# A convolution that stores the first image of its first pair in two halves

## The chip, the cores and the metric

The kernel runs on one core of one Trainium2 chip. The metric is the device time of one execution, in microseconds (us), less being better. A profiled execution is shown by its span (from the first to the last instruction that the profiler records) and its own device time, which is a little longer than the span.

## What is computed

A 3x3 convolution with a border of zeros: 16 images of 64 channels and 64 x 64 pixels in float32, 128 output channels.

```
x_pad = np.pad(x, ((0, 0), (0, 0), (1, 1), (1, 1)))
output[b, co] += weight[co, ci, kh, kw] * x_pad[b, ci, kh:kh+h, kw:kw+w]     # for all b, co, ci, kh, kw
```

The input is 16 MB, the output 32 MB.

## The kernel before

The images go through in eight **pairs** (`NP`, loop in line 128). A pair fills the 128 partitions: image 0 of the pair has its 64 channels on partitions 0 to 63, image 1 on 64 to 127. Each pair has four **blocks** (line 138) of 8 row pairs, that is, 16 output rows. The row direction uses a short (Winograd) form: the sum of two neighbouring input rows, made beforehand into `ss`, goes through the middle weights once and serves an even and an odd output row. A block therefore has three groups of matmuls in float16 on TensorE (line 168): U from `ss`, A and Bt from the rows themselves in `xs`. ScalarE copies U out of PSUM into `ut` (line 182); VectorE adds A and U into the even output rows (line 190), then Bt and U into the odd ones (line 193), for image 0 first and image 1 second. The result lies in `ot`, one float32 tile of 2 MB for each image.

**Loads.** SyncE issues the weights and the first three pairs as raw float32 (x0, x1, x2; lines 41 to 47, 2 MB each) before anything else. ScalarE and GpSimd cast them to float16 (line 98): x1 during pair 0, x2 piece by piece during pair 1. GpSimd issues the loads of pairs 3 to 7 itself (`load`, line 58), cast on the way from 2 MB of float32 to 1 MB of float16: pairs 3 and 4 early (line 108), pairs 5 to 7 after its sums for pair 2 (line 134). It also makes the sums for each next pair (line 131).

**Stores.** `cuts_of[p]` (line 120) says for each pair, and for each of its two images, after which block which rows are stored: `whole` means all 64 rows after block 3, `halves` means rows 0 to 31 after block 1 and rows 32 to 63 after block 3. Before the change all pairs use `whole` but the last, which uses `halves` for both images. Image 0 is stored by SyncE straight away (line 195). Image 1's store is put on a list, `held`, and issued by ScalarE after its copies of a later block (line 185).

**Queues.** SyncE's transfers (weights, x0 to x2, stores of image 0) share DMA queue 1, in order of issue; ScalarE's stores go through queue 10; GpSimd's casting loads through queue 0. All run on the same 16 DMA engines. On each engine's instruction stream a store waits for the addition that finishes its rows, and the instructions behind it wait with it. SyncE has nothing behind its loads but the stores.

**Buffers.** `opool` has seven 2 MB buffers, which the raw tiles x0 to x2 and the output tiles take in turn. Eight semaphores serve SyncE's and ScalarE's transfers in turn.

Of the kernel before, what the change touches and what calls it, by code (L numbers as in the profile page):

```python
# [13 lines left out]
def kernel(  # L14
# [10 lines left out]
    NP = B // 2  # L25
# [91 lines left out]

    whole = {3: (0, 64)}
    halves = {1: (0, 32), 3: (32, 64)}
    cuts_of = [(whole, whole)] * (NP - 1) + [(halves, halves)]  # L120

    def store(eng, p, b2, ot, lo, hi):
        return eng.dma_start(
# [106 lines left out]
```

## Time and profile before

| | |
|---|---|
| median of 3 runs | 126.69 us (126.62 to 126.82) |
| the profiled execution's own time | 126.58 us |
| its span | 124.8 us |
| TensorE busy | 107.9 us (86% of the span) |
| VectorE busy | 84.6 us (68%) |
| ScalarE busy | 46.5 us (37%) |
| GpSimd busy | 37.5 us (30%) |
| HBM read and written | 17.07 MB and 33.55 MB |
| stores of 2 MB, from issue to landing | median 18.4 us (SyncE), 19.9 us (ScalarE) |
| stores of 1 MB, from issue to landing | median 10.6 us (SyncE), 11.0 us (ScalarE) |

How to read the profile: PE is TensorE, DVE VectorE, ACT ScalarE, POOL GpSimd, SP SyncE; "L193" is line 193 of the kernel. `out<-in` names the tile written and the tile read. "DMA" rows give the busy share of the 16 DMA engines in tenths and the GB/s that landed; a casting load lands half the bytes that it reads. The chain of waits follows the work that ended last back to the start, the timeline lists instructions in order of time (equal ones merged), and the table of stretches gives, for each stretch of time, the busy time and number of instructions of each engine, TensorE's granted clock, the DMA engines' share and the GB/s.

### The profile page before, as it was taken

Reading aid. Unit: us, or ns where it says so; the run is one execution under the profiler, and the core shown is the slowest. Engines: PE = TensorE matmul, PEld = TensorE weight load, DVE = VectorE, ACT = ScalarE, POOL = GpSimd, SP = SyncE. Lnnn points to the kernel's source line nnn. Section 1 sums busy time; section 2 is a strip of 40 time slices with the busy share of each in tenths; the row PEclk is TensorE's granted clock in tenths of the full one; section 3 lists DMA queues with packets and bytes.
Section 4 is the critical chain, followed back from the end, with each engine's and each line's share of the span. In section 5 each row is a group of like instructions: output and inputs, shape, how many; then the busy total and the mean of one; then the engine's idle time right before and its main releaser. Section 6 shows DMA issues by size and latency. Waiting matters only on the chain.

```text
span 124.8 us, 2423 instructions
## 1 busy us (share of the span) xinstructions
PE 107.9 (86%) x984; PEld 49.8 (40%) x984; DVE 84.6 (68%) x135; ACT 46.5 (37%) x78; POOL 37.5 (30%) x28
## 2 busy tenths in 40 slices
PE   0599999999999999999999999999999999990000
PEld 0444444444444444444444444444444444440000
DVE  1019977878877887877777778777877787774000
ACT  4118549966663332433333333333333333330000
POOL 2219780799990006600093002900000000000000
PEclk9999999999999999999999999999999999999555
DMA  4999999999999999999999999999999999999991
GB/s 113 406 425 446 441 315 257 213 155 410 352 352 349 349 378 357 352 344 347 386 339 362 344 357 431 425 436 436 415 425 431 431 425 436 425 415 417 423 407 63
DMA packets 3898, 45.52 MB, mean 365 GB/s; under 512 B 432, under 2 KB 432, under 8 KB 560
## 3 DMA queue, kind: packets, MB, share of 16 engines
q1 hardware_dynamic: 1872, 23.36, 44.7%
q10 hardware_dynamic: 1296, 16.78, 31.7%
q0 software_dynamic: 720, 5.24, 20.8%
q8 instruction: 7, 0.11, 0.3%
q14 instruction: 3, 0.02, 0.0%
HBM read 17.07 MB, written 33.55 MB: 406 GB/s over the span
## 4 chain that ended last, share of the span: by engine, by line
PE 86%; DMA 2%; DVE 1%; issue 1%; POOL 1%; DVEq 0%
PE acc L168 81%; PE warm L91 3%; DMA w_raw<-in_weight_dram 2%; PE wp L85 1%; DVE ot L190 1%; POOL w L52 1%; DVEq L225 0%; DVE ot L193 0%; DVEq L190 0%
## 5 line engine op out<-in xcount | busy, mean ns | idle before, releaser
L168 PE MATMUL acc<-xs,Wt 64*128 64x504 f16 (+3 forms) x768 | 87.0, 373 | 0.0
L168 PEld LDWEIGHTS <-Wt 64*128 64x128 f16 x960 | 46.8, 94 | 56.2 <-issue 0.8
L182 ACT COPY ut<-acc 128x512 f32<-128x512 f32 x64 | 34.4, 589 | 57.1 <-issue 39.3
L190 DVE TENSOR_TENSOR ot<-acc,ut 128x512 f32<-128x512 f32 x64 | 41.2, 685 | 20.9 <-PE acc L168 18.6
L193 DVE TENSOR_TENSOR ot<-acc,ut 128x512 f32<-128x512 f32 x64 | 41.1, 683 | 0.0
L67 POOL TENSOR_TENSOR ss<-xs 128x1024 f16<-128x1024 f16 x10 | 21.0, 2127 | 31.5 <-DMA xs<-in_x_dram 31.2
L168 PE MATMUL acc<-ss,Wt 64*128 64x504 f16 (+1 forms) x192 | 26.0, 377 | 0.0
L98 ACT CAST xs<-x 128x1024 f16<-128x1024 f32 (+1 forms) x10 | 10.5, 1069 | 3.0 <-DMA x<-in_x_dram 3.0
L67 POOL TENSOR_TENSOR ss<-x 128x1024 f16<-128x1024 f32 x4 | 9.4, 2361 | 5.0 <-DMA x<-in_x_dram 5.0
L67 DVE TENSOR_TENSOR ss<-x 128x512 f16<-128x512 f32 x4 | 3.3, 868 | 7.5 <-DMA x<-in_x_dram 7.5
L85 PE MATMUL wp<-ident,w 128*64 128x128 f16 x18 | 1.3, 328 | 4.6 <-POOL w L52 4.6
L98 POOL CAST xs<-x 128x1024 f16<-128x1024 f32 (+1 forms) x2 | 3.0, 1518 | 4.2 <-DMA x<-in_x_dram 4.2
L91 PE MATMUL warm<-blank 128*128 128x400 f32 x6 | 4.1, 854 | 0.0
L85 PEld LDWEIGHTS <-w 128*64 128x64 f16 x18 | 1.1, 209 | 4.6 <-POOL w L52 4.6
L58 POOL DMA_DIRECT2D xs<-in_x_dram x5 | 2.9, 578 | 0.0
L91 PEld LDWEIGHTS warm<-blank 128*128 128x128 f32 x6 | 1.8, 328 | 1.4 <-issue 1.3
L92 ACT CAST Wt<-wp 128x384 f16<-128x384 f32 x1 | 0.5, 479 | 3.3 <-PE wp L85 3.3
L92 ACT ACT_TABLE_LOAD x1 | 1.3, 1283 | 0.7 <-PEq L214 0.7
L52 POOL CAST w<-w_raw 128x576 f16<-128x576 f32 x1 | 0.7, 662 | 2.6 <-DMA w_raw<-in_weight_dram 2.6
L88 DVE MEMSET blank<- 128x400 f32 x1 | 0.4, 392 | 0.9 <-PEq L214 0.9
L103 ACT CAST Wt<-wp 128x384 f16<-128x384 f32 x1 | 0.5, 478 | 0.5 <-DVE Wt L95 0.5
L94 DVE TENSOR_TENSOR Wt<-wp,Wt 128x384 f16<-128x384 f32 x1 | 0.6, 550 | 0.0
(8 smaller groups left out, 1.9 us busy)
## 6 DMA issues: line engine op xcount, KB each, us to landing
out_dram<-ot SPq DMA_DIRECT2D x7, 2048.0 KB, 18.4
out_dram<-ot ACTq DMA_DIRECT2D x7, 2048.0 KB, 19.9
x<-in_x_dram SPq DMA_DIRECT2D x3, 2048.0 KB, 12.0
xs<-in_x_dram POOLq DMA_DIRECT2D x5, 1024.0 KB, 20.4
out_dram<-ot SPq DMA_DIRECT2D x2, 1024.0 KB, 10.6
out_dram<-ot ACTq DMA_DIRECT2D x2, 1024.0 KB, 11.0
w_raw<-in_weight_dram SPq DMA_DIRECT2D x1, 288.0 KB, 3.1
```

The costliest lines, as they stand in the source:

```text
L52: keep(nc.gpsimd.tensor_copy(w16, w_raw))
L58: keep(nc.gpsimd.dma_start(xs[p], x_rows[128 * p : 128 * p + 128, :, :]))
L67: eng.tensor_add(ss[p][:, lo : lo + n, :], v[:, lo : lo + n, 0, :], v[:, lo : lo + n, 1, :])
L85: nc.tensor.matmul(wp[q : q + 64, k * CO : k * CO + CO], w16[:, t::9], ident)
L91: nc.tensor.matmul(warm[:, 0:400], blank[:, 0:128], blank)
L92: keep(nc.scalar.copy(wrow(G1), wps[1]))
L94: keep(nc.vector.tensor_sub(wrow(G21), wps[2], wrow(G1)))
L98: keep(copy(xs[p][:, lo:hi, :], src[:, lo:hi, :]))
L168: nc.tensor.matmul(tiles[b2][:, lo - j0 : hi - j0, c_lo:c_hi], Wt[p0 : p0 + 64, wi, kw, :], rhs, start=i == 0, stop=i == n - 1,)
L182: keep(nc.scalar.copy(ut, U[b2]))
L190: nc.vector.tensor_add(ots[b2][:, j0 : j0 + RB, 0, :], A[b2], us[b2])
L193: nc.vector.tensor_add(ots[b2][:, j0 : j0 + RB, 1, :], Bt[b2], us[b2])
```

## The change

```
     whole = {3: (0, 64)}
     halves = {1: (0, 32), 3: (32, 64)}
-    cuts_of = [(whole, whole)] * (NP - 1) + [(halves, halves)]
+    cuts_of = [(halves, whole)] + [(whole, whole)] * (NP - 2) + [(halves, halves)]
```

For pair 0, image 0, line 195 now issues two stores from SyncE: rows 0 to 31 after block 1 and rows 32 to 63 after block 3, 1 MB each, in place of one store of 2 MB after block 3. Image 1 of pair 0 and all other pairs are stored as before.

## The prediction

> **What bounds the kernel now.** The chain of waits comes first, because it names what ended last among the engines. Its last pieces:
>
> ```profile
> 9.94 101.39 PE acc L168 x948
> ...
> 113.27 0.60 DVE ot L193
> ```
>
> Columns: start, length, what. TensorE works without a hole from 9.94 to 112 us, and VectorE ends at 113.27 + 0.60 = 113.9 us. But the span is 124.8 us: for 10.9 us no engine works. The page's 40 slices say what does:
>
> ```profile
> DVE  1019977878877887877777778777877787774000
> ...
> DMA  4999999999999999999999999999999999999991
> GB/s 113 406 425 446 441 315 257 213 155 410 352 352 349 349 378 357 352 344 347 386 339 362 344 357 431 425 436 436 415 425 431 431 425 436 425 415 417 423 407 63
> ```
>
> The DMA engines are busy from the second slice to the last but one, through the four slices (of 3.1 us) in which VectorE is idle. Is that full speed? Section 3 of the page gives the bytes:
>
> ```profile
> q0 software_dynamic: 720, 5.24, 20.8%
> ...
> HBM read 17.07 MB, written 33.55 MB: 406 GB/s over the span
> ```
>
> The five casting loads (line 58, queue 0) read 10.49 MB and land 5.24 MB, and the GB/s row counts what lands. So where queue 0 runs alone, 215 GB/s stands for 430 read. The stretches of the trace (DMA share and GB/s are the last two columns; PE busy and count come first):
>
> ```profile
> 22.00:25.00 3.00, 3.00 (x34) 1.38 (x32) 2.40 (x5) 2.80 (x5) 2.40 (x2) 1.00 1.05 218
> 25.00:28.00 3.00, 3.00 (x30) 1.36 (x28) 2.34 (x4) 1.85 (x4) 3.00 (x3) 1.00 1.01 153
> 28.00:30.00 2.00, 2.00 (x22) 0.92 (x20) 1.94 (x4) 0.77 (x2) 2.00 (x3) 1.00 1.04 393
> 114.00:120.00 6.00, 0.00 (x0) 0.00 (x0) 0.00 (x0) 0.00 (x0) 0.00 (x0) 0.61 1.02 431
> ```
>
> At 22 to 25 us, 218 landed is 436 read: full. In the end stretch only stores move, at 431: full. 17.07 + 33.55 = 50.62 MB at 431 GB/s is 117.4 us. So **the bytes bound the kernel**, and the remaining 7.4 us of the span are the start, the ragged end (410, 295 and 123 GB/s in the microseconds 120 to 123) and one hole: 25 to 28 us, where 153 GB/s land although the DMA share is 1.01. Its price: (218 - 153) x 3 us = 0.195 MB landed, 0.39 MB read, over 0.431 = **0.9 us**.
>
> What is that hole? Not lack of work: between 27.5 and 28.5 us the trace has 18 more packets of queue 0, and that queue's share stays at 99.3% in 25 to 28 us, with 54 packets where 22 to 25 us had 96. The packets take longer. What is new is the first store:
>
> ```profile
> 23.66 13.15 SPq L123 DMA_DIRECT2D out_dram<-ot  x2
> ```
>
> ```profile
> q0 software_dynamic: 54, 0.44, 99.3%
> q1 hardware_dynamic: 1, 0.02, 1.3%
> ```
>
> The first row (SyncE's issues; two merged, the first at 23.66 us) starts the first 2 MB store; the others (queues in 25 to 28 us: packets, MB, share) show that 4 us later it has written one packet. All packets slow down about 2 us after the first store's issue and recover as its packets appear. ScalarE's first store, issued at 26.86 us, brings no second hole: 28 to 30 us lands 393, with loads among it. I read the hole as the price of the first store into otherwise pure load traffic, paid once.
>
> **The change, part by part.** It removes one 2 MB store (issue 23.66 us) and adds two of 1 MB. No other instruction moves: the order on PE, DVE, ACT and POOL is the same; SyncE has one store more, and the waits that guard reused DMA semaphores shift by one place.
>
> *Issue.* The first half needs the last addition into rows 0 to 31 of image 0, in block 1. VectorE's two additions of line 193 there start at 16.48 us and take 1.29 us; the first, image 0's, ends near 17.1. The store now follows its addition (22.95 + half of 1.28 = 23.6) by under 0.1 us, so the first half issues at about **17.2 us, 6.5 us earlier**; the second stays at 23.66. One more issue costs SyncE 0.33 us, which waits up to 21.1 us between stores: nothing. The shifted semaphores cost nothing either: one is taken again after eight transfers, at the shortest from 75.5 to 113.9 us, and a store lands 25.5 us after its issue at the latest. Behind the waiting first half on SyncE stand only the other stores, all due later. The next one due is the second half, 6.5 us later.
>
> *Queue.* All loads of line 47 and before are already issued, so the first half stands behind the rest of image pair x2 on queue 1. x2 lands at 22.5 us (GpSimd's sums of it start at 22.60 after 4.23 us of waiting), so the half writes from about 21 us on, beside queue 0. In 16 to 19 us queues 0 and 1 moved 42 and 38 packets: they take turns. The half is 128 rows of 8 KB, 8 packets for each of 16 engines; one turn of both is 0.31 + 0.62 us (16 KB at 431/16 GB/s = 0.61), eight turns 7.4 us, so it ends near 28.5 us. The second half is at work by 27.8 (23.66 + 4.1, as the store now). There is no time without a store after that.
>
> *What it displaces.* The 1 MB takes 1.05 / 431 = 2.4 us from loads 3 and 4. Load 3's first user starts at 28.85 us; load 4's at 33.31, after a wait of 0.23 us for TensorE and none for the load. If POOL is 2.4 us late there, nothing follows: its sums for pair 4 are used after 60 us, and it waits 10.3 us for its next load anyway. If the hole falls on x2's last packets, they land up to 2.4 us later, about 25 us; ScalarE's cast of x2 now starts at 24.54, and ScalarE idles 1.15 us before its next copy. That hides it; without that cover TensorE would slip by 1 to 2 us, against the 8 us of stores that are queued at 114 us (6 us at 431 and 4.8 us at 172 GB/s are 3.4 MB). Output buffers come free earlier or as now; VectorE waits for no DMA in the list of waits.
>
> *At the end.* The queue holds the same bytes, at the same rate. Bytes moved out of 23 to 42 us into 21 to 28 us let later ones advance, but only by what the hole gives back. Bounds for that: 0 if the first store costs its hole wherever it stands; 0.9 us if all of it goes. I take 0, because the hole begins with the store and not with a lack of packets. The two halves' smaller packets cost: the last four stores are 1 MB too, and 114 to 120 us runs at 431, against 426 in 90 to 114 with mostly 2 MB stores: 0. Sum: 126.58 (the profiled execution: 124.8 of span and 1.78 around it) + 0 = **126.6 us**; the median of the three runs is 126.69, 0.1 higher.
>
> The Trainium skill speaks against the change: "DMA: Bandwidth & Descriptors", section "Bandwidth", measures 341 GB/s for a 1 MB transfer and 425 for 16 MB, and says to batch to 1 MiB or more. By its 341, two halves would cost 2 x (1.05/0.341 - 1.05/0.431) = 1.3 us, an estimate giving 127.9. The trace's 431 GB/s over 1 MB stores disagrees as long as other transfers are queued beside them, as they are here.
>
> **The rivals.**
>
> *A. The hole closes.* With x2 still on queue 1 and a second queue of loads, the first store's start-up is covered, or 8 KB packets fill the path sooner. For it: other queues later start and stop without a hole (38 to 42 us: 336 to 360 GB/s with casts among it). Against: queue 0 had packets in the hole and did not use it. Time: 126.58 - 0.9 = 125.7; half closed 126.1. Chance 0.28.
>
> *B. Slower: the start-up is paid twice.* If the first half does not take turns but runs through, it ends at 21 + 8 x 0.31 = 23.5 us, and the second half writes only from 27.8: four microseconds without a store, then a fresh start at the same 0.9 us. It decides at the point where the first half's last packet leaves before 27.8 us. Time 127.5. For it: the second half's issue stays at 23.66. Against: the 42-to-38 turns. Chance 0.14.
>
> *C. Slower: an added store costs its fixed time.* The weight load takes 3.11 us for 0.29 MB, which at 431 is 0.7: 2.4 us fixed. Uncovered, 129.0 us. Against: the 431 of the end stretch. Chance 0.06.
>
> *D. The half does not get out early*, held behind x2 until the second is due: no effect, 126.6; it counts with the forecast.
>
> **How the numbers follow.** Forecast with D 0.52: 126.6, own range 126.2 to 127.0, as the 16 engines end raggedly over 2 us and another order of packets may shift the last one by a few tenths. A measurement tells about 0.2% (0.25 us) from no change; of the 0.52 I put 0.05 on either side beyond that. Faster: 0.28 + 0.05 = 0.33. Same: 0.42. Slower: 0.05 + 0.14 + 0.06 = 0.25. The range takes in A and B whole, 125.6 to 127.6, and leaves out C and little else.
>
> **What would show it.** SyncE's first store at 17.2 us. A stretch of about 2.5 us from 19 to 22 us landing well under the mix's full rate, and 25 to 28 us filled: the hole moved (forecast). No such stretch anywhere: A. Two: B. VectorE's end at 113.9 us should not move; if the end stretch is under 425 GB/s, C. I am wrong if the last store lands much earlier or later than now while no hole has changed.

## The result, and the profile after

The changed kernel takes 126.36 us (median of 22 runs, 126.17 to 127.19); the kernel before, on the same chips, 126.71 us (22 runs). The ratio is **0.9971, 95% interval 0.9960 to 0.9983**: 0.35 us faster, a little more than the 0.25 us that a measurement tells from no change. The forecast was 126.6 us and no change; the range 125.6 to 127.6 holds the time. The one profiled execution does not show the gain: it took 126.58 us with a span of 124.8 us, exactly as before. So the traces say where time moved, and only the times of many runs say how much. Here and below a median goes over all runs of a kernel, a ratio over its fast ones alone (those within 1.5% of its fastest).

The page of the changed kernel, share and rate of the DMA engines in 40 slices:

```profile
DMA  5999999999999999999999999999999999999991
GB/s 131 394 431 452 441 302 229 284 284 289 365 349 336 341 381 349 365 344 336 373 362 365 334 347 415 441 436 420 415 447 415 436 410 441 431 402 418 425 407 53
```

The slices of 155 and 213 GB/s are gone, and 229 is now the lowest of that region. The stretches (the last two columns are DMA share and GB/s), of the kernel before, whose lines for 22 to 28 us stand in the prediction:

```profile
20.00:22.00 2.00, 2.00 (x22) 0.94 (x20) 1.27 (x3) 1.73 (x4) 0.00 (x0) 1.00 0.97 205
```

and of the changed kernel:

```profile
20.00:22.00 2.00, 2.00 (x22) 0.89 (x18) 1.27 (x3) 1.73 (x4) 0.00 (x0) 1.00 0.96 180
22.00:25.00 3.00, 3.00 (x32) 1.48 (x30) 2.40 (x5) 2.80 (x5) 2.70 (x2) 1.00 1.03 292
25.00:28.00 3.00, 3.00 (x32) 1.38 (x28) 2.44 (x4) 1.86 (x4) 3.00 (x3) 1.00 1.03 287
```

The hole has moved from 25 to 28 us to about 20 to 22 us (180 GB/s, still mostly casting loads, where 205 landed before), and 25 to 28 us is filled: 0.42 MB of casts, which read 0.84, and 0.44 MB of stores are 1.28 MB in 3 us, 427 GB/s. SyncE's stores and VectorE's last addition:

```profile
17.46 6.64 SPq L123 DMA_DIRECT2D out_dram<-ot  x2
```

```profile
113.38 0.60 DVE ot L193
```

The first half is issued at 17.46 us, the second 6.3 us later, and VectorE ends at 113.98 us (before: 113.87). The pair x2 is not later: GpSimd's sums of it start at 22.30 us (22.60 before).

How much of the hole is left? In a fixed stretch, 18 to 29 us, the traffic can be added up from the queues, casting queue 0 twice, because it reads twice what lands. The kernel before (packets, MB landed, share):

```profile
q0 software_dynamic: 244, 1.81, 86.8%
q1 hardware_dynamic: 56, 0.66, 14.4%
q8 instruction: 1, 0.02, 0.5%
```

and the changed kernel:

```profile
q0 software_dynamic: 198, 1.49, 69.4%
q1 hardware_dynamic: 180, 1.39, 31.3%
q8 instruction: 1, 0.02, 0.5%
```

That is 2 x 1.81 + 0.66 + 0.02 = 4.30 MB before and 2 x 1.49 + 1.39 + 0.02 = 4.39 MB after. 11 us at 431 GB/s would be 4.74 MB. The loss falls from 1.02 to 0.81 us (the stretch has other small losses besides the hole).

### The profile page after: what moved, and what is told of

The parts are those of the page before. It is cut to its first block, busy times and chain, and to the rows that moved or that the text cites. A ratio compares the mean times of both kernels' runs of the same rounds, so it can differ in the third digit from the quotient of the medians.

```text
span 124.8 us, 2427 instructions
## 1 busy us (share of the span) xinstructions
PE 107.6 (86%) x984; PEld 50.2 (40%) x984; DVE 84.5 (68%) x135; ACT 46.5 (37%) x78; POOL 37.5 (30%) x28
## 4 chain that ended last, share of the span: by engine, by line
PE 81%; DMA 6%; DVE 2%; issue 1%; DVEq 0%; SPq 0%
PE acc L168 81%; DMA x<-in_x_dram 6%; DVE ot L190 1%; DVE ss L67 1%; DVE ot L193 0%; DVEq L225 0%; SPq L41 0%; DVEq L190 0%
## 5 line engine op out<-in xcount | busy, mean ns | idle before, releaser
L168 PEld LDWEIGHTS <-Wt 64*128 64x128 f16 x960 | 47.3, 94 | 56.2 <-issue 1.1
## 6 DMA issues: line engine op xcount, KB each, us to landing
x<-in_x_dram SPq DMA_DIRECT2D x3, 2048.0 KB, 12.3
```

The lines of the kernel that those rows point to most:

```text
L168: nc.tensor.matmul(tiles[b2][:, lo - j0 : hi - j0, c_lo:c_hi], Wt[p0 : p0 + 64, wi, kw, :], rhs, start=i == 0, stop=i == n - 1,)
```

## The experiments

Ratios are against runs of the kernel before on the same chip. "Traffic" is the sum just shown, for 18 to 29 us, from the one profile of each run.

| kernel | first store issued, its packets | median, us | ratio (95%) | traffic, MB |
|---|---|---|---|---|
| before, first profile | 23.7 us, 16 KB | 126.71 | | 4.30 |
| before again | 23.8 us, 16 KB | 126.66 | 0.9998 (0.9980 to 1.0017) | 4.36 |
| late halves, kept late | 23.6 us, 8 KB | 126.78 | 1.0009 (0.9998 to 1.0020) | 4.32 |
| warm store | as before, and 64 KB at 1.0 us | 126.73 | 0.9999 (0.9980 to 1.0018) | 4.25 |
| after | 17.5 us, 8 KB | 126.36 | 0.9971 (0.9960 to 0.9983) | 4.39 |
| after again | 17.2 us, 8 KB | 126.35 | 0.9983 (0.9958 to 1.0008) | 4.40 |
| late halves, first try (in fact early) | 17.4 us, 8 KB | 126.35 | 0.9971 (0.9952 to 0.9989) | 4.41 |
| half by ScalarE | 17.2 us, 8 KB | 126.39 | 0.9988 (0.9967 to 1.0008) | 4.43 |
| both images in halves | 17.4 and 18.0 us, 8 KB | 126.44 | 0.9970 (0.9951 to 0.9989) | 4.33 |
| early whole | 5.6 us, in the queue behind x2, 16 KB | 126.34 | 0.9984 (0.9969 to 0.9998) | 4.32 |
| small first | 14.8 us, 16 rows after block 0, 4 KB | 126.56 | 0.9990 (0.9972 to 1.0008) | 4.44 |

**Late halves.** Is it the smaller packets or the earlier place?

```
-                store(nc.sync, p, 0, ots[0], *cuts_of[p][0][blk])
+                if p == 0:
+                    store(nc.sync, p, 0, ots[0], 32, 64)
+                    store(nc.sync, p, 0, ots[0], 0, 32)
+                else:
+                    store(nc.sync, p, 0, ots[0], *cuts_of[p][0][blk])
```

> The first image of pair 0 is stored in two halves, both issued after block 3 (rows 32 to 63 first). Packets of 8 KB as in the changed kernel, but the time of the kernel before. The hole at the first store cost 0.9 us of DMA time in the kernel before and 0.6 in the changed one. If the smaller packets shrink it: hole 0.6 us, time about 126.4. If the earlier place behind x2 shrinks it: hole 0.9 us, time 126.7 as before.

Measured 126.35 us, but the experiment failed: the scheduler moved the half whose rows were done to the front of SyncE's list, and it was issued at 17.4 us. It is a second copy of the changed kernel, and repeats its gain.

**Late halves, kept late.** The same with `keep(...)` around both stores, which fixes their order.

> Both halves of the first image issued near 23.8 us, after block 3, in fixed order: packets of 8 KB at the place of the kernel before. If the packet size shrinks the hole: 0.55 us instead of 0.9, at 25 to 28 us, time 126.35. If the early place shrinks it: 0.9 us, time 126.7.

Measured 126.78 us, and SyncE's row now starts late:

```profile
23.64 0.82 SPq L123 DMA_DIRECT2D out_dram<-ot  x2
```

No gain. Packets of 8 KB at the old place do nothing; **the early place is needed**.

**Warm store.** Is the hole the price of the first store that the DMA engines ever make?

```
+    first = const.tile([128, 2 * W], F32)
+    keep(nc.gpsimd.memset(first, 0.0))
+    nc.scalar.dma_start(out_rows[0, :, 0:2, :], first.rearrange("p (r c) -> p r c", c=W))
```

> The kernel before, with one added store of 64 KB (zeros, 512 bytes on each of 128 partitions, into rows 0 and 1 of image 0, overwritten later) issued by ScalarE at about 1 us, ahead of the loads. If the hole is paid once, by the first store that each DMA engine ever makes, it is gone at 25 to 28 us and the time is 125.8 to 126.0. If it is the start of a stream of stores among loads, whatever was stored earlier, it stays at 0.9 us and the time is 126.7 to 126.9 (64 KB more).

Measured 126.73 us, the hole where it was (4.25 MB of traffic, 1.14 us lost). So a small store 22 us earlier does not take the hole away. That it belongs to the start of the stream of stores is the reading that is left, not something this run shows by itself.

**Early whole.** The early place with 16 KB packets: a tile of zeros is stored in place of image 0 of pair 0, whose own result is left out. It is issued at 5.6 us and queued behind x2. To make room, the input pool has six buffers, and the last casting load is issued at 36.3 us; these lines are not shown.

```
+    keep(nc.vector.memset(zeros, 0.0))
+    nc.sync.dma_start(out_rows[0, :, :, :], zeros)
...
+                if p > 0:
+                    store(nc.sync, p, 0, ots[0], *cuts_of[p][0][blk])
```

> A store of 2 MB in packets of 16 KB directly behind x2 on queue 1, the changed kernel's place with the old packet size. It stores zeros in place of the first image of pair 0, whose own result is not stored; the input pool has six buffers, so that the zeros fit, and the last casting load is issued some 8 us later. If the packet size sets the hole: 0.9 us at 20 to 25 us, time 126.7. If the place sets it: 0.55 us, time 126.35.

The time follows the place (126.34 us, ratio 0.9984), the traffic does not (4.32 MB, as in the kernel before). By the time, the place sets it, though the interval (0.9969 to 0.9998) is barely clear of no change and the later casting load is a second difference; by the trace, the hole was hardly smaller: 0.80 us lost in 20 to 25 us, where the kernel before lost 0.91 in 25 to 29. Its deepest microsecond is 20 to 21 us (82 GB/s), about 15 us after the store was issued: the hole does not come at a fixed time after the issue.

**Half by ScalarE.** Does it matter that the half stands behind x2 on queue 1? An edit of the changed kernel:

```
+                if (p, blk) == (0, 1):
+                    held.append((0, 0, ots[0], 0, 32))
+                else:
+                    store(nc.sync, p, 0, ots[0], *cuts_of[p][0][blk])
```

> The changed kernel, with the first half issued by ScalarE near 18 us on queue 10 instead of by SyncE behind x2 on queue 1. If what counts is that a store starts some 6 us earlier, among loads of two queues: time 126.35, as in the changed kernel. If it is the place behind x2 on the same queue: 126.7, as in the kernel before.

The median is 126.39 us and the traffic 4.43 MB, as in the changed kernel; the interval (0.9967 to 1.0008) does not shut out no change. The queue seems not to matter. Queue 1's own first store, issued at 23.5 us here, brings no hole: 25 to 28 us moves 2 x 0.39 + 0.40 + 0.10 = 1.28 MB, 427 GB/s. So in this run the hole goes with the first store of all and not with the first on each queue.

**Both images in halves.**

```
+    cuts_of = [(halves, halves)] + [(whole, whole)] * (NP - 2) + [(halves, halves)]
```

> Both images of pair 0 go in halves; image 1's first half is issued by ScalarE near 21 us instead of 26.9. If bytes stored earlier are worth something, 126.1 or less; if only the hole at the first store counts, it is 0.6 us as in the changed kernel and the time is 126.35.

126.44 us, the same gain, and no more from a second megabyte early. The hole is as large as in the kernel before, 0.96 us in 20 to 25 us.

**Small first store.**

```
+    cuts_of = [({0: (0, 16), 3: (16, 64)}, whole)] + [(whole, whole)] * (NP - 2) + [(halves, halves)]
```

> The first image goes in 16 rows after block 0 (packets of 4 KB) and 48 rows after block 3 (12 KB). If only the first store's packet size counts, a hole of 0.3 us and a time of 126.1. If the rest of the hole is paid when larger packets follow, 0.6 to 0.9 us in sum and 126.4 to 126.7. The slow drain of the four quarters (133.8 us) should not come back, since only 24 packets less wait in turn: 16 per engine in all, as with halves.

126.56 us, between the two kernels and clear of neither. Its trace has two small holes, one at each start, and the same traffic in sum as the changed kernel (4.44 MB).

**Quarters.**

```
+    quarters = {n: (16 * n, 16 * n + 16) for n in range(4)}
+    cuts_of = [(quarters, whole)] + [(whole, whole)] * (NP - 2) + [(halves, halves)]
```

> The first image of pair 0 goes in four quarters of 16 rows after each block (packets of 4 KB, the first issued near 14.7 us). If the packet size sets the hole: 0.9 at 16 KB, 0.6 at 8 KB, so 0.3 to 0.45 at 4 KB, time 126.1 to 126.2. If the place behind x2 sets it: as in the changed kernel, 0.6 us and 126.35. If each small store has a price of its own, slower than the changed kernel by some tenths.

133.84 us, ratio 1.0493 (1.0433 to 1.0553): by the ratio 6 us slower, which none of the three expectations had. The queues in 32 to 52 us (packets, MB, share):

```profile
q0 software_dynamic: 248, 1.90, 45.3%
q10 hardware_dynamic: 243, 3.72, 43.8%
q1 hardware_dynamic: 241, 0.95, 12.6%
```

The three queues moved nearly the same number of packets, whatever a packet holds: they take turns packet by packet. Queue 1, with 4 KB packets against 16 KB, gets a quarter of queue 10's bytes. So the last quarter, issued at 24 us, is down only at 57.6 us, as the chain of waits and VectorE's timeline say (this kernel's line 191 is line 190 of the kernel before):

```profile
24.00 33.57 DMA out_dram<-ot
```

```profile
57.69 1.29 DVE L191 TENSOR_TENSOR ot<-acc,ut 128x512 f32<-128x512 f32 x2 [7.51 <-DMA out_dram<-ot]
```

Pair 3's output tile takes over that buffer. VectorE waits 7.5 us for it, and TensorE, behind VectorE, 4.5 us.

**Quarters with eight buffers.** An attempt to take that wait away: `opool` with 8 buffers, `xpool` with 6.

> The four quarters that cost 7 us, with eight output buffers instead of seven (and six input buffers instead of eight, so that they fit; the last casting load is issued later). If the loss was VectorE's 7.5 us wait for the buffer whose small packets drained late, the wait is gone and the time is 126.2 to 126.5. If small packets as such are slow, it stays at 130 or more.

132.91 us, ratio 1.0343 (1.0304 to 1.0383). The wait did not go (line 193 here is line 190 of the kernel before):

```profile
DVE ot L193 <- DMA out_dram<-ot: 6.1, 1, 6.1
```

VectorE's timeline has one addition of that line at 50.63 us and the second at 57.37 us: the late buffer went to the other image of the same pair 3, one addition later. That the buffer is the whole loss is thus supported by the chain, not shown by taking it away.

**Fewer bytes.** The base of the prediction was that bytes set the end. Of the first image of pair 4 only rows 0 to 31 are stored, so this kernel's output is incomplete:

```
+                lo, hi = cuts_of[p][0][blk]
+                store(nc.sync, p, 0, ots[0], lo, 32 if p == 4 else hi)
```

> The kernel before, but of image 0 of pair 4 only rows 0 to 31 are stored (1.05 MB less; its other rows are left out of the output). If the bytes bound the kernel, as the prediction had it, the time falls by 1.05 MB / 431 GB/s = 2.4 us to 124.3. If the arithmetic or the last stores alone set the end, it stays at 126.7.

125.34 us, ratio 0.9888 (0.9856 to 0.9921): 1.35 us of the expected 2.4. The rest is seen in the stretches. This kernel, then the kernel before:

```profile
98.00:102.00 4.00, 4.00 (x42) 1.87 (x40) 3.02 (x5) 1.22 (x3) 0.00 (x0) 1.00 0.76 320
```

```profile
98.00:102.00 4.00, 4.00 (x42) 1.85 (x38) 2.83 (x5) 1.41 (x3) 0.00 (x0) 1.00 1.03 434
```

320 against 434 GB/s: the DMA engines ran dry until pair 6 was stored, at 100.3 us. (434 - 320) x 4 us / 431 GB/s = 1.06 us, which is what 2.4 - 1.35 leaves. From about 76 us, when the loads are through, a pair brings 4.2 MB of stores every 12.8 us, which the queues move in 9.7: they eat up a backlog, and at 100 us there is little over a microsecond of it left. The DMA engines and the arithmetic are nearly in balance there.

The end shows it too. The kept traces hold sixteen landings for each transfer, as many as there are DMA engines (27 transfers and 432 landings in the kernel before). Those of the last store lie between 121.58 and 123.78 us in the kernel before; with fewer bytes, fifteen of them lie between 121.31 and 121.64 and one at 122.20. The latest come 1.6 us earlier, the earliest only 0.3 us: the saved bytes help where a backlog was left.

**The two kernels again**, unchanged, for second profiles:

> The changed kernel once more, for a second profile and more times. If the hole is truly smaller there: 0.5 to 0.6 us between 20 and 25 us, time 126.35. If the first profile was chance: up to 0.9 us.

> The kernel before once more, for a second profile and as the test of the comparison itself: ratio 1.000 within 0.1%, hole 0.75 to 1.1 us between 25 and 29 us.

126.35 and 126.66 us: the difference repeats, though this interval alone (0.9958 to 1.0008) would not prove it. The second profile of the changed kernel loses 0.52 us in 20 to 25 us, as expected (the first 0.64); that of the kernel before loses 0.68 us in 25 to 29 us, less than the 0.75 to 1.1 expected (the first 0.91). Traffic was 4.40 and 4.36 MB: the second profile of the kernel before lost less than its first, so one profile's hole is uncertain by some 0.15 us. In the end stretch, 114 to 120 us, the two profiles of the kernel before land 431 and 422 GB/s, those of the changed kernel 422 and 426.

## Why the prediction was right or wrong

- *Order and issue*: right. 17.46 us against 17.2 forecast, VectorE's end moved by 0.11 us, SyncE's additional issue cost nothing. The half landed 12.3 us after its issue, at 29.8 us, against an end near 28.5 forecast from turns.
- *Displaced loads*: right. x2 and loads 3 and 4 held up nobody.
- *The hole begins with the store*: right. It followed the store from 25 to 28 us to 20 to 22 us. A small store long before does not remove it (warm store). The delay of about 2 us after the issue, which the prediction read from one store, is not fixed: in the early whole store it is about 15 us.
- *The hole costs the same wherever it stands ("I take 0")*: **the step that failed**, as a size. Taken over the profiles, the four of early halves (after, after again, first try, half by ScalarE) have a mean traffic of 4.41 MB in 18 to 29 us, the two of the kernel before and the late halves 4.33: 0.08 MB or 0.2 us less lost; with the warm store among the late ones, 4.31 and 0.2 us. The fewer-bytes kernel, which is the same program as the kernel before up to pair 4, has 4.21 in that stretch; with it the late ones have 4.29, and the difference is 0.3 us. The medians say 0.35 us; the ratios of the four early runs (0.9971, 0.9983, 0.9971, 0.9988) are gains of 0.15 to 0.37 us, 0.28 in the mean. The bounds given, 0 to 0.9 us, hold it, and it lies between the forecast and rival A's half-closed hole (0.5 us).
- *The 8 KB packets*, named under rival A as a reason, are not enough: late halves gained nothing.
- *Rival B* (two starts): no second hole; 25 to 28 us is at 287 GB/s with casts among it, and the half was still draining when the second arrived. *Rival D* (the half held back): it was issued at 17.46 us and landed at 29.8. *Rival C* (a fixed price for each store): both images in halves have two more stores and the same gain. By the sign named for C, under 425 GB/s in the end stretch, the changed kernel's 422 would have spoken for it; but the kernel before shows 422 in its second profile too, so that sign was too fine.
- *Smaller packets cost nothing*: true of two halves, wrong as a rule. The turns between queues that the prediction used to place the half (42 to 38 packets) already held the price that the quarters paid.
- *The bytes bound the kernel*: only in part. The fewer-bytes run shows that it holds for about the first 1.3 us of savings; past them the queues run dry at 100 us.

What stays open: why an early start is worth about 0.3 us. A smaller hole accounts for 0.2 to 0.3 us in the four kernels with an early half, within an uncertainty of the same size. But both images in halves and the early whole store gained about as much with traffic of 4.33 and 4.32 MB, as in the kernel before.

The order in which the 16 DMA engines finish could hold the rest, and the landings of the last store bear on that. In the kernel before (two profiles) and the late halves, the mean of the sixteen is 122.51 us and the last 124.06; in the four with an early half, 122.37 and 123.70. So the mean comes 0.14 us earlier and the last, which ends the kernel, 0.36 (0.19 without the late halves, whose last is at 124.40). In both images in halves and the early whole store the mean is that of the kernel before (122.48 and 122.57), yet the last comes at 123.66 and 123.50. That fits a gain that lies partly in a more even finish. It is not shown: the last landings of two profiles of one kernel differ by 0.2 us, and no run changed the finish alone.

No run that stores the whole result beat the changed kernel by more than its interval.

## What to carry to other kernels

Where the DMA engines are busy to the end, add up the bytes per stretch (a casting load counts at what it reads) before trusting a busy share: a hole can stand at a share of 1.01. A store issued earlier gained only what its place gave back, here about 0.3 us, and a saving in bytes ended where the queues ran dry between batches of stores. Cutting a store into smaller rows gives its queue a smaller part of the bandwidth beside queues with larger rows; check when the buffer behind it is needed again.

## What the runs showed of the hardware

- Queues with work waiting shared the DMA engines by packets, not by bytes: 248, 243 and 241 packets in 20 us, with 4 KB packets on one and 16 KB on another, so that 0.95 MB moved beside 3.72.
- When stores start among loads, the engines lose traffic for about 2 to 3 us while their busy share stays near 1; a 64 KB store 22 us earlier does not prevent it (4.25 MB in 18 to 29 us against 4.30). In 25 to 28 us of the kernel before, 153 GB/s land at a share of 1.01, where 218 landed in the 3 us before.
- Stores of 1 MB run as fast as those of 2 MB when others are queued beside them: 422 to 431 GB/s at 114 to 120 us, against 424 to 426 in 90 to 114 us.
